# Attention of a two-layer backbone: a projection group moved to a scores bank, the context weights transposed ahead of the value products, all weight parts copied through SBUF in units with value products, and the head norms put off by a unit

## The chip, the cores and the metric

The kernel runs on one core of a Trainium2 chip. Its engines are TensorE (PE; its weight loads are listed as PEld), VectorE (DVE), ScalarE (ACT), GpSimd (POOL) and SyncE (SP), which issues the DMAs. Each has its own instruction stream and works it off in order; semaphores tie the streams together. The metric is the time of one execution on the device in microseconds (us), as the median of several runs.

## The reference

Two layers over 1024 latent tokens and 256 context tokens of width 1024. Layer 0 mixes tokens with differential attention, layer 1 with a state-space scan; each is followed by a dense MLP. The change touches layer 0's attention alone. For each of 8 heads there are two components c of width 64, and the two softmaxes are subtracted:

```python
s = einsum('bqhcd,bkhcd->bhcqk', q, k)
p = softmax(s, axis=-1)
w = p[:, :, 0] - lam * p[:, :, 1]
o = einsum('bhqk,bkhe->bqhe', w, v)
return rmsnorm(o, subln_g) * (1.0 - lambda_init)
```

q and k of the latent tokens are rotated (axial rotary) after their projections. Latent queries read all 1280 keys, context queries only the 256 context keys. All arithmetic is float32; the kernel multiplies in halves, hi and lo, with three products for one (`mm3`, L132 to L134).

## The kernel before, in words

**Tiling.** `phase_b` walks through 72 units (h, u): 8 heads of 9 units. In u=0 both 128-token tiles of context queries are done against 256 keys, in u=1 to 8 one latent tile each against 1280 keys. Around the units the order of TensorE, VectorE, ScalarE and GpSimd is the order in which the code is written (`manual_schedule`); the DMAs on SP are placed by a planner.

**One unit.** TensorE computes the scores of both components into PSUM banks 0 to 4 (`scores`, L510; L504 in u=0). VectorE copies each component to SBUF and takes its maximum on the way (`maxima`, L523; L519 in u=0; the instruction works with negated scores, so its accumulator is a minimum). ScalarE takes the exponentials with their sums (`exps`, L533; L530 in u=0), component 0 in a double buffer, component 1 in a single one. VectorE then forms w from both (`combine`, L541 to L544). One unit later TensorE transposes w in three parts, of 4, 2 and 4 key tiles (`w_part`, L556; for the context unit one part of 4 transposes, L551): part 0 into bank 5, part 1 into the upper half of bank 6, part 2 into bank 5 where the unit has a projection group and bank 7 where not. `w_evac` brings a part to SBUF as hi and lo: directly (ScalarE copies hi out of PSUM, L564; VectorE subtracts for lo out of PSUM, L565), or by one ScalarE copy to SBUF (L569, a ring of three buffers) from which GpSimd makes hi (L570) and lo (L571). Before, part 0 went the direct way, and parts 1 and 2 the other.

**Values.** Two units of latent tiles make a pair. Its value products (`values`, 30 matmuls of 256 columns; 6 for the context pair) into bank 6 stand right behind the scores of the unit two after the pair's last one: u=2 for the context pair and u=4, 6, 8 and the next head's u=1 for the four latent pairs. Those four are called late units here: the products read the weights that the unit's own parts are about to overwrite, so all three parts are evacuated only behind `combine`. `pair_out` (L652) copies the product out at the unit's end.

**Projections.** The next head's K and Q are projected in groups (`proj_group`) beside the units: two groups in u=0 (context keys, then the first latent keys), one each in u=2, 3, 5 and 7. All go to bank 7. Of u=0's two, the first is computed whole ahead of the scores and leaves bank 7 by ScalarE and VectorE (L451, L452); other groups' matmuls are spread between the transposes. A latent group has five further steps: `evac` (L456, L457, and four DMAs that swap rows), a step of nothing, `sine` (GpSimd, L462), `add` (VectorE, L465), `store` (ScalarE L137 and VectorE L138, both helpers that others use too, and two DMAs). Two steps are taken per unit, one in the middle (ahead of component 1's exponentials) and one at the end.

**Norms.** The rows of a finished head are normalised while the next one runs: `norm_load` fetches a pair's outputs and its broadcast row scales by two DMAs (tiles W, from od and rsd) at a unit's start, and `norm_pair` scales them at the unit's end (VectorE L684), splits them (ScalarE L137, GpSimd L138) and stores both halves. That is done in u=6, 7, 8 and the next head's u=0 and 1, from head 1's u=6 to head 7's u=1, with one set of buffers.

## Time and profile before

| | us |
|---|---|
| Median of three runs | 3051.51 (3049.69 to 3059.32) |
| The profiled execution's own time | 3048.01 |
| Its span on the core | 3046.2 |
| Heads and units of attention | from about 242 to 910 |

The mean granted TensorE clock is 0.978. The page's 40 slices are 76 us each; attention fills slices 4 to 12. The four heads between 425 and 760 us repeat each other closely, about 83 us per head, and head 4 (from its u=0 near 551 us) stands for them. In the tables of waits, a row reads: engine, tile and line that waited, the engine, tile and line whose end released it, total us, how many times, the longest. In a timeline, a row has its start, its length, engine, line, operation, output tile and input tile, shapes and count, and in square brackets the idle time of the engine before it with what ended that. A wait that depends on several things is put down to the one that came last.

### The profile page before, as it was taken

How to read it: one execution, taken by the hardware profiler on the slowest of the kernel's cores; microseconds unless marked ns; L12 is line 12 of the kernel's file. 1: busy time of each engine (PE TensorE's matmuls, PEld its weight loads, DVE VectorE, ACT ScalarE, POOL GpSimd, SP SyncE). 2: the span in 40 equal slices, each digit the busy share in tenths (PEclk: the TensorE clock that was granted, in tenths of full speed). 3: DMA queues.
4: the chain of work that ended last, by engine and by line, in shares of the span. 5: the costliest groups of instructions: out<-in, count | busy, mean ns of one | idle time of the engine just before them, and what ended most of it. 6: DMA issues, size and time to landing. Idle time of an engine off the chain costs nothing.

```text
span 3046.2 us, 42172 instructions
## 1 busy us (share of the span) xinstructions
PE 2855.1 (94%) x15376; PEld 2368.6 (78%) x15376; DVE 1909.6 (63%) x2766; ACT 1256.1 (41%) x2254; POOL 814.1 (27%) x794
## 2 busy tenths in 40 slices
PE   6998999999799999999999999688999899999998
PEld 4687888878687877788777778588787778888887
DVE  5357877777654654344677755899543666666555
ACT  3425555555544643333422222467344533222223
POOL 2314665666654400000100003566112200000003
PEclk9999999999899999999999999899999999999999
DMA  9955556556716455532666663577642221111113
GB/s 264 304 174 164 150 161 167 164 161 173 245 57 197 125 169 174 166 119 93 199 192 184 185 196 104 159 213 206 214 148 95 66 66 56 52 49 52 56 39 135
DMA packets 384235, 448.83 MB, mean 147 GB/s; under 512 B 54694, under 2 KB 299676, under 8 KB 382876
## 3 DMA queue, kind: packets, MB, share of 16 engines
q1 hardware_dynamic: 384028, 446.14, 49.1%
q8 instruction: 121, 1.98, 0.3%
q14 instruction: 86, 0.70, 0.1%
HBM read 320.88 MB, written 120.95 MB: 145 GB/s over the span
## 4 chain that ended last, share of the span: by engine, by line
PE 66%; DVE 10%; DMA 8%; issue 5%; ACT 4%; POOL 4%; SPq 3%; DVEq 0%; POOLq 0%; ACTq 0%
PE PS L132 19%; PE PS L134 19%; PE PS L133 19%; SPq L80 3%; PE PS L510 2%; ACT F L533 1%; PE PS L202 1%; DVE F L523 1%; DVE FD L1708 1%; PE PS L556 1%; PE PS L1690 1%; PE PS L1725 1%; DMA W<-rsd 1%; DVE FD L1699 1%; DVE R L138 1%
## 5 line engine op out<-in xcount | busy, mean ns | idle before, releaser
L132 PE MATMUL PS<-H,R 128*128 128x512 f32 (+1 forms) x960 | 361.3, 378 | 15.5 <-ACT F L569 13.8
L133 PE MATMUL PS<-H,R 128*128 128x512 f32 (+1 forms) x992 | 366.1, 369 | 2.9 <-POOL H L138 2.8
L134 PE MATMUL PS<-H,R 128*128 128x512 f32 (+1 forms) x960 | 348.9, 368 | 0.1
L133 PE MATMUL PS<-R,H 128*128 128x512 f32 x692 | 271.0, 392 | 0.0
L132 PE MATMUL PS<-R,H 128*128 128x512 f32 x676 | 268.2, 400 | 2.0 <-ACT R L137 1.6
L134 PE MATMUL PS<-R,H 128*128 128x512 f32 x676 | 260.1, 392 | 1.1 <-DVE H L138 1.1
L132 PE MATMUL PS<-R 128*128 128x256 f32 (+1 forms) x656 | 221.9, 339 | 7.0 <-ACT R L137 2.8
L132 PEld LDWEIGHTS PS<-H,R 128*128 128x128 f32 x960 | 184.3, 192 | 50.3 <-ACT F L569 15.2
L137 ACT ACTIVATE R<-W 128x512 fp32r<-128x512 f32 (+1 forms) x203 | 154.6, 766 | 161.1 <-PE PS L133 112.0
L1625 POOL TENSOR_SCALAR stat<-stat 128x1 f32<-128x1 f32 x24 | 14.9, 620 | 765.4 <-ACT PS L1623 765.1
L133 PE MATMUL PS<-R 128*128 128x256 f32 (+1 forms) x624 | 208.6, 334 | 9.1 <-DVE R L565 9.1
L1428 DVE TENSOR_TENSOR F<-PS,F 128x1024 f32<-128x1024 f32 (+1 forms) x113 | 136.4, 1212 | 128.3 <-PE PS L134 128.1
L133 PEld LDWEIGHTS PS<-H,R 128*128 128x128 f32 x992 | 191.4, 193 | 31.1 <-POOL H L138 3.6
L138 DVE TENSOR_TENSOR R<-W,R 128x512 fp32r<-128x512 f32 (+1 forms) x162 | 140.5, 872 | 114.5 <-ACT R L137 75.2
L134 PEld LDWEIGHTS PS<-H,R 128*128 128x128 f32 x960 | 184.3, 192 | 32.6 <-issue 2.1
L533 ACT ACTIVATE F<-F,stat 128x1280 f32<-128x1280 f32 x128 | 174.4, 1362 | 84.5 <-DVE F L523 84.2
L523 DVE TENSOR_SCALAR_CACHE_REDUCE F<-PS 128x1280 f32<-128x1280 f32 x128 | 185.1, 1483 | 8.6 <-PE PS L510 8.3
L570 POOL TENSOR_SCALAR R<-F 128x256 fp32r<-128x256 f32 (+1 forms) x128 | 124.2, 970 | 169.3 <-ACT F L569 147.5
L134 PE MATMUL PS<-R 128*128 128x512 f32 (+1 forms) x488 | 168.4, 354 | 0.0
L132 PE MATMUL PS<-H 128*128 128x512 f32 x408 | 161.0, 395 | 1.5 <-ACT H L137 1.5
L134 PE MATMUL PS<-H 128*128 128x512 f32 x408 | 159.4, 392 | 0.0
L510 PE MATMUL PS<-R,R 128*128 128x512 f32 x720 | 155.3, 364 | 0.4 <-DVE F L523 0.4
(426 smaller groups left out, 7037.8 us busy)
## 6 DMA issues: line engine op xcount, KB each, us to landing
W<-in_mlp_w SPq DMA_DIRECT2D x148, 256.0 KB
W<-in_mlp_w SPq DMA_DIRECT2D x68, 512.0 KB
FU<-in_ada_w SPq DMA_DIRECT2D x40, 512.0 KB
W<-in_ada_w SPq DMA_DIRECT2D x32, 512.0 KB
H<-hidd SPq DMA_DIRECT2D x64, 256.0 KB
W<-in_s_w_glu SPq DMA_DIRECT2D x64, 256.0 KB
hidd<-FU SPq DMA_DIRECT2D x52, 256.0 KB
recd<-FD SPq DMA_DIRECT2D x48, 256.0 KB
```

The source lines that it names most:

```text
L80: return self.nc.sync.dma_start(out=out, in_=in_)
L132: mm(out, ah, bh, start=first, stop=False, **kw)
L133: mm(out, ah, bl, start=False, stop=False, **kw)
L134: mm(out, al, bh, start=False, stop=last, **kw)
L137: self.nc.scalar.activation(hi, src, AF.Copy)
L138: (lo_eng or self.nc.vector).tensor_tensor(lo, src, hi.bitcast(F32), ALU.subtract)
L202: self.nc.tensor.matmul(acc[32 * j : 32 * j + 32, 0:256], self.scT[:, 2 * k : 2 * k + 32], w[:, 256 * j : 256 * j + 256], start=k == 0, st ...
L510: mm(self.PS[:, 1280 * c + k0 : 1280 * c + k1], Q[:, c, r, qs], K[c][:, k0:k1], start=r == 0, stop=r == 1)
L523: ts(p[c], self.PS[:, 1280 * c : 1280 * c + 1280], 1.0, None, ALU.mult, ALU.min, accum_out=sm[:, c : c + 1])
L533: nc.scalar.activation(p[c], p[c], AF.Exp, bias=sm[:, c : c + 1], scale=-1.0, accum_out=sn[:, 0:1] if c else s0[:, u + 1 : u + 2])
L570: nc.gpsimd.tensor_scalar(hi, t, 1.0, 0.0, ALU.mult, ALU.add)
L1428: nc.vector.tensor_tensor(acc[:, n : n + m], y[:, n : n + m], acc[:, n : n + m], ALU.add)
```

## The change

It has five parts.

1. In u=0 the first of the two projection groups is computed into bank 4, the last of the scores banks, in place of bank 7 (`proj_group` takes the bank as an argument).
2. In u=1, where w of the context unit is transposed (`first`), the transposes stand ahead of the 30 value products, the evacuation is direct, and it is placed right behind these products in the order, ahead of the exponentials.
3. In the other late units (u=4, 6, 8) part 0 also goes by one ScalarE copy and GpSimd (`part == 0 and (first or not late)`).
4. The empty step of a latent group is gone, and a step that was at a unit's end is put in `later` and taken in the next unit right behind the maxima. So `sine` comes at the next unit's middle, `add` behind the maxima of the unit after it, and `store` at that unit's middle. 
5. `norm_pair` also goes to `later`: behind the maxima of the next unit, behind a waiting `add`. `norm_load` moves from the unit's start to behind that.

TensorE, ScalarE and SP run the same number of instructions as before. On VectorE 24 subtractions (L565, 128x512) are gone; on GpSimd 24 pairs L570 and L571 of 128x512 are added. A few instructions of the output projection, behind attention, stand in another order, by the planner.

In the rows below, F_1811 is the buffer of w and its copies, R_98 and R_1810 hold rounded operands, FC the projection's and the norms' scratch, W the norms' and weights' staging, stat and lamc small columns, PS PSUM.

VectorE at u=2 of head 4, before, from the norm's scaling at the end of u=1 to the maxima of u=3:

```order
L684 SCALAR_TENSOR_TENSOR W<-W,lamc 128x256
L523 TENSOR_SCALAR F_1811,stat<-PS 128x1280 x2
L565 TENSOR_TENSOR R_98<-PS,R_98 128x4x128
L465 TENSOR_TENSOR FC<-FC 128x512
L541 RECIPROCAL stat<-stat 128x1
L542 SCALAR_TENSOR_TENSOR stat<-FC,stat,lamc 128x1
L544 SCALAR_TENSOR_TENSOR F_1811<-F_1811,stat 128x1280
L138 TENSOR_TENSOR R_98<-FC,R_98 128x512
L457 SCALAR_TENSOR_TENSOR FC<-PS,W 128x512
L523 TENSOR_SCALAR F_1811,stat<-PS 128x1280 x2
```

and now, from the maxima of u=2 to the end of that unit:

```order
L523 TENSOR_SCALAR F_1811,stat<-PS 128x1280 x2
L465 TENSOR_TENSOR FC<-FC 128x512
L684 SCALAR_TENSOR_TENSOR W<-W,lamc 128x256
L565 TENSOR_TENSOR R_98<-PS,R_98 128x4x128
L138 TENSOR_TENSOR R_98<-FC,R_98 128x512
L541 RECIPROCAL stat<-stat 128x1
L542 SCALAR_TENSOR_TENSOR stat<-FC,stat,lamc 128x1
L544 SCALAR_TENSOR_TENSOR F_1811<-F_1811,stat 128x1280
L457 SCALAR_TENSOR_TENSOR FC<-PS,W 128x512
```

The norm's L684 was ahead of the two maxima and is behind them, with the group's `add` (L465) ahead of it; the direct subtraction L565 comes behind both, and the store's L138 has moved from behind `combine` (L544) to ahead of it.

ScalarE from u=8 of head 3 to the exponentials of u=0 of head 4, before:

```order
L137 ACTIVATE W<-W 128x256
L533 ACTIVATE F_1811,FC<-F_1811,stat 128x1280
L533 ACTIVATE F_1811,stat<-F_1811,stat 128x1280
L564 ACTIVATE R_98<-PS 128x4x128
L569 ACTIVATE F_1811<-PS 128x256
L569 ACTIVATE F_1811<-PS 128x512
L652 ACTIVATE FC<-PS 128x256
L137 ACTIVATE W<-W 128x256
L451 ACTIVATE R_98<-PS 128x256
L564 ACTIVATE R_98<-PS 128x4x128
L530 ACTIVATE F_1811,FC<-F_1811,stat 128x256 x2
```

and now:

```order
L137 ACTIVATE W<-W 128x256
L533 ACTIVATE F_1811,FC<-F_1811,stat 128x1280
L533 ACTIVATE F_1811,stat<-F_1811,stat 128x1280
L569 ACTIVATE F_1811<-PS 128x512
L569 ACTIVATE F_1811<-PS 128x256
L569 ACTIVATE F_1811<-PS 128x512
L652 ACTIVATE FC<-PS 128x256
L451 ACTIVATE R_98<-PS 128x256
L137 ACTIVATE W<-W 128x256
L564 ACTIVATE R_98<-PS 128x4x128
L530 ACTIVATE F_1811,FC<-F_1811,stat 128x256 x2
```

Part 0 of u=8 is now an L569 like its neighbours, and the copy of the first group (L451) is ahead of the norm's L137 in place of behind it. The norm's L137 still stands ahead of the next exponentials, but it now reads what VectorE makes behind the maxima.

TensorE in u=1 of head 4, before, the last three value products, the context transposes and the next scores:

```order
L132 MATMUL PS<-R_98 128x256
L133 MATMUL PS<-R_98 128x256
L134 MATMUL PS<-R_98,R_1810 128x256
L551 MATMUL PS<-ident,F_1811 128x128 x4
L510 MATMUL PS<-R_1810,R_98 128x512 x4
L510 MATMUL PS<-R_1810,R_98 128x256 x4
L510 MATMUL PS<-R_1810,R_98 128x512 x4
L132 MATMUL PS<-R_98 128x256
```

and now, the end of u=0, the scores of u=1, the transposes and the first value products:

```order
L134 MATMUL PS<-H,R_98 128x512
L510 MATMUL PS<-R_1810,R_98 128x512 x4
L510 MATMUL PS<-R_1810,R_98 128x256 x4
L510 MATMUL PS<-R_1810,R_98 128x512 x4
L551 MATMUL PS<-ident,F_1811 128x128 x4
L132 MATMUL PS<-R_98 128x256
L133 MATMUL PS<-R_98 128x256
L134 MATMUL PS<-R_98,R_1810 128x256
```

The four transposes of the context weights (L551) have moved from behind the thirty value products to ahead of them.

The whole diff:

```diff
--- before.py
+++ after.py
@@ -428,11 +428,11 @@
 
         return split
 
-    def proj_group(self, h, T, g, wt):
+    def proj_group(self, h, T, g, wt, b=None):
 
         nc = self.nc
         n, c0 = self.G_TOK[g], (256, 768, 0)[g]
-        b = self.qb.next()[:, 0:n]
+        b = (self.qb.next() if b is None else b)[:, 0:n]
         scale = 1.0 if T else -0.125
         t = slice(c0 - 256, c0 + 256)
         hT = self.hT[g]
@@ -468,7 +468,7 @@
             self.split(s[:, 0], s[:, 1], qc)
             out()
 
-        return [product(k) for k in range(8)], [direct] if g == 2 else [evac, None, sine, add, store]
+        return [product(k) for k in range(8)], [direct] if g == 2 else [evac, sine, add, store]
 
 
     def lam_setup(self):
@@ -599,7 +599,7 @@
                 for f in post:
                     f()
                 rest[0]()
-                post = rest[2:]
+                post = rest[1:]
                 yield
         for f in post:
             f()
@@ -786,7 +786,7 @@
             if f:
                 f()
 
-        ready = []
+        ready, later = [], []
 
         def evac():
             while ready:
@@ -800,8 +800,6 @@
                 pv = todo.pop(0)[1:] if todo and todo[0][0] == n else None
                 late = pv and pv[1]
                 parts = 3 if prev and prev[1] else 1 if prev else 0
-                if front and n - 6 >= 9 and (n - 6) % 9 < 5 and (n - 6) // 9 < 7:
-                    norm_load((n - 6) // 9 - 1, (n - 6) % 9)
                 if h == 7 and u > 5:
                     load6(u)
                 if front:
@@ -816,7 +814,8 @@
                     if u % 2 == 0 and u < 8 and (h, pair + 1) not in loaded:
                         load_q(h, pair + 1)
                     if h < 7:
-                        groups = [self.proj_group(h + 1, *a, wts[a[0]]) for a in self.AHEAD.get(u, ())]
+                        ahead = self.AHEAD.get(u, ())
+                        groups = [self.proj_group(h + 1, *a, wts[a[0]], self.bank(4) if a != ahead[-1] else None) for a in ahead]
                     if len(groups) == 2:
                         for f in groups[0][0] + groups[0][1]:
                             f()
@@ -826,6 +825,10 @@
                         load_q(h + 1, 0)
                         load_q(h + 1, 1)
                     self.maxima(u, p, sm)
+                while later:
+                    later.pop(0)()
+                if front and n - 6 >= 9 and (n - 6) % 9 < 5 and (n - 6) // 9 < 7:
+                    norm_load((n - 6) // 9 - 1, (n - 6) % 9)
                 if front:
                     if h < 7:
                         if u == 0:
@@ -839,14 +842,17 @@
                     fills = [groups[0][0][i : i + 2] for i in (0, 2, 4)]
                 elif groups:
                     fills = [groups[-1][0][i:j] for i, j in (((0, 4), (4, 8), (8, 8)) if u == 3 else ((0, 3), (3, 6), (6, 8)))]
-                if pv:
+                first = parts == 1
+                if pv and not first:
                     values(*pv)
                 for part in range(3):
                     if part < parts:
                         tb = pb[:, 256:512] if part == 1 else self.bank(7 if part == 2 and not groups else 5)
                         t = self.w_part(prev[1], prev[2], part, tb)
-                        ready.append((*t, part == 0))
-                    if not late or part == 2:
+                        ready.append((*t, part == 0 and (first or not late)))
+                    if pv and first and part == 0:
+                        values(*pv)
+                    if not late or first or part == 2:
                         evac()
                     if part == 1:
                         next_post()
@@ -872,7 +878,8 @@
                     sums.append((n + 1, lambda a=pv: pair_sums(*a)))
                     if pv[0] == 7:
                         tail.append((n + 1, pv[1]))
-                next_post()
+                if post:
+                    later.append(post.pop(0))
                 if groups:
                     rest = groups[-1][1]
                     rest[0]()
@@ -894,7 +901,7 @@
                     elif u == 5:
                         norm_rows(h - 1)
                 if h < 8 and n - 6 >= 9 and (n - 6) % 9 < 5 and (n - 6) // 9 < 7:
-                    norm_pair((n - 6) // 9 - 1, (n - 6) % 9)
+                    later.append(lambda a=((n - 6) // 9 - 1, (n - 6) % 9): norm_pair(*a))
                 if n == 72:
                     self.raw = Ring([self.wv(8, 1024), self.wv(12, 1024)])
                     self.wo_raws = [self.wo_load(3, 0), self.wo_load(0, 1)]
```

## The prediction

> **What bounds the kernel now.** I read the table of TensorE's waits, that of 425 to 760 us (four heads), then the timelines of head 4. TensorE's waits that the change aims at, over the whole execution:
>
> ```profile
> PE PS L556 <- DVE R L565: 20.3, 14, 2.9
> PE PS L132 <- ACT F L569: 13.8, 6, 2.6
> ...
> PE PS L133 <- DVE R L565: 9.1, 6, 2.4
> ...
> PE PS L659 <- ACT F L569: 6.4, 1, 6.4
> ```
>
> Together 49.6 us: no removal of these waits is worth more. In head 4 they are found at u=0's first group, the context pair's values in u=2, and part 0 in u=5:
>
> ```profile
> 551.25 0.39 PE L132 MATMUL PS<-H,R 128*128 128x256 f32 x1 [2.54 <-ACT F L569]
> ...
> 573.93 0.39 PE L133 MATMUL PS<-R 128*128 128x256 f32 x1 [1.21 <-DVE R L565]
> ...
> 601.21 0.66 PE L556 MATMUL PS<-ident,F 128*128 128x128 f32 x4 [1.54 <-DVE R L565]
> ```
>
> The second thing to see is how little room the softmax leaves. In four heads VectorE waited 20.8 us for the norm's row scales, and its maxima 0.7 for scores:
>
> ```profile
> DVE W L684 <- DMA W<-rsd: 20.8, 11, 3.2
> ...
> DVE F L523 <- PE PS L510: 0.7, 4, 0.2
> ```
>
> So maxima, exponentials, `combine` and the next maxima form a chain as long as TensorE's work. The starts of the first maximum in u=8 of head 3, and in u=0, 1, 2, 3, 7 and 8 of head 4:
>
> ```profile
> 545.57 1.48 DVE L523 TENSOR_SCALAR_CACHE_REDUCE F<-PS 128x1280 f32<-128x1280 f32 x1
> ...
> 556.68 0.41 DVE L519 TENSOR_SCALAR_CACHE_REDUCE F<-PS 128x256 f32<-128x256 f32 x1
> ...
> 566.78 1.48 DVE L523 TENSOR_SCALAR_CACHE_REDUCE F<-PS 128x1280 f32<-128x1280 f32 x1
> ...
> 577.33 1.49 DVE L523 TENSOR_SCALAR_CACHE_REDUCE F<-PS 128x1280 f32<-128x1280 f32 x1
> ...
> 585.69 1.48 DVE L523 TENSOR_SCALAR_CACHE_REDUCE F<-PS 128x1280 f32<-128x1280 f32 x1
> ...
> 617.79 1.48 DVE L523 TENSOR_SCALAR_CACHE_REDUCE F<-PS 128x1280 f32<-128x1280 f32 x1
> ...
> 628.86 1.48 DVE L523 TENSOR_SCALAR_CACHE_REDUCE F<-PS 128x1280 f32<-128x1280 f32 x1
> ```
>
> The steps are 11.11, 10.10, 10.55, 8.36, 32.10 (four units) and 11.07 us, 83.3 together. I work the change out as new lengths of these steps.
>
> **The change part by part.** The pieces of a plain step, from u=4, and one L465 of each length, the long one with the GpSimd row beside it:
>
> ```profile
> 594.13 1.48 DVE L523 TENSOR_SCALAR_CACHE_REDUCE F<-PS 128x1280 f32<-128x1280 f32 x1
> 597.06 1.37 ACT L533 ACTIVATE F<-F,stat 128x1280 f32<-128x1280 f32 x1
> 600.47 0.68 DVE L565 TENSOR_TENSOR R<-PS,R 128x512 fp32r<-128x512 f32 x1
> 596.95 0.68 DVE L465 TENSOR_TENSOR FC<-FC 128x512 f32<-128x512 f32 x1
> 621.58 1.77 DVE L465 TENSOR_TENSOR FC<-FC 128x512 f32<-128x512 f32 x1 [0.29 <-POOL FC L462]
> 621.50 1.30 POOL L138 TENSOR_TENSOR R<-W,R 128x512 fp32r<-128x512 f32 x1
> ```
>
> The first exponential starts about 1.52 behind the first maximum's start, the second 1.41 later (597.06), and w is done 3.41 after that, as L565 follows it: 6.34. Both maxima take 2.82 (594.13 to 596.95). Now the norm around u=2:
>
> ```profile
> 576.92 0.49 DVE L684 SCALAR_TENSOR_TENSOR W<-W,lamc 128x256 f32<-128x256 f32 x1 [3.05 <-DMA W<-rsd]
> 577.49 0.42 ACT L137 ACTIVATE W<-W 128x256 fp32r<-128x256 f32 x1 [5.51 <-DVE W L684]
> 577.82 0.58 ACT L564 ACTIVATE R<-PS 128x512 fp32r<-128x512 f32 x1
> 582.62 0.64 ACT L137 ACTIVATE R<-FC 128x512 fp32r<-128x512 f32 x1
> 583.87 1.10 DVE L138 TENSOR_TENSOR R<-FC,R 128x512 fp32r<-128x512 f32 x1
> 544.23 1.42 DVE L684 SCALAR_TENSOR_TENSOR W<-W,lamc 128x256 f32<-128x256 f32 x1
> ```
>
> From L684's start to the end of ScalarE's copy: 0.90. Before, this ran ahead of the maxima, and the first exponential lay beside the second maximum. Now ScalarE, in order, holds the norm's copy ahead of the exponentials, and that copy needs L684 behind both maxima. The first exponential starts 2.82 + 0.90 = 3.72 behind the first maximum, 2.20 later than in a plain step; an `add` ahead of L684 costs 0.68 more, a direct copy (L564) behind it 0.58. This is the price of part 5; its return is that the norm and its wait for row scales leave the stretch ahead of the maxima. Step by step, in us:
>
> - u=8 to u=0, 11.11. 3.72 + 1.41 + 3.41, and 0.4 for the direct group's subtraction: 8.9, **−2.2**. Bank 4 pays here: the 2.54 for bank 7 go, since u=8's maxima are over at 548.4 (545.57 + 2.82) and TensorE could start at 548.7 (551.25 − 2.54).
> - u=0 to u=1, 10.10. L684 and the store's L138 (0.5 and 1.1) leave its end; `add`, L684, L137 and L564 delay its exponentials. 8.7 with short lengths, 10.7 where L465 and L684 take 1.77 and 1.42: **−0.4**, between.
> - u=1 to u=2, 10.55. 3.72 + 0.58 + 1.41 + 3.41 = 9.1: **−1.4**; the 3.05 for row scales go. Part 2 takes the 1.21 off TensorE here, but it then stands at u=2's part 0 until u=1's w is done, so it counts nothing by itself.
> - u=2 to u=3, 8.36. 3.72 + 0.68 + 0.58 + 1.41 + 3.41, between the exponentials 0.64 for the store's copy and 0.3 for a part's, and 0.6 for the cosine product: 11.3, **+3.0**.
> - u=3 to u=7, 32.10. No norm. In u=4 the store's copy now waits for `add`: 2.82 + 0.68 + 0.64 + 3.41 = 7.55, 0.4 less than now, as part 3 takes a 0.68 subtraction away from behind w; u=6's end loses such a subtraction and L684 (0.68 + 0.4). TensorE's work takes part of it: **−1.5**. The 1.54 at u=5 shrinks by those 0.68, no further, as w is late.
> - u=7 to u=8, 11.07. As u=2: 11.3; with GpSimd busy under L465 and L684 2.0 more: **+1.0**, half of it.
>
> Sum −1.5 per head. Bounds: all short −3.9 (−2.2, −1.35, −1.4, +3.0, −2.1, +0.2), all long +2.4 (−1.7, +0.6, −0.9, +3.0, −0.8, +2.2). I take the middle, as L465 shows both lengths.
>
> Part 3's GpSimd work is, in each of 24 units, one more pair like
>
> ```profile
> 784.06 0.62 POOL L570 TENSOR_SCALAR R<-F 128x512 fp32r<-128x512 f32 x1
> 784.77 1.29 POOL L571 TENSOR_TENSOR R<-F,R 128x512 fp32r<-128x512 f32 x1
> ```
>
> 1.9 us, about 46 in all. I cost it at nothing beyond the lengths above: its weights are read two units later, and `sine` moves ahead of it out of the same queue. If that cover fails, u=6's and u=8's values wait about 1 us each, which the upper bound holds.
>
> The moved steps pass other queues. `sine` now stands on GpSimd ahead of its unit's part copies and waits there for four row swaps; L570 and L571 queue behind it, for weights that are read a unit or more later, and I cost it at nothing for the same reason. On ScalarE everything of the unit queues behind the norm's copy: direct copy, exponentials, L569, `pair_out`; on VectorE, behind L684, the direct subtraction that frees bank 5 for part 2, and `combine`. On SP a norm is two stores and two loads:
>
> ```profile
> SPq L80 <- POOL W L138: 22.7, 8, 5.3
> ```
>
> SP stood 22.7 us before the lo stores, with swaps and query loads behind them, as GpSimd's L138 came last in its unit. Now L138 stands ahead of the unit's parts, and the row scales' load, which needs only L684, ahead of both stores. So I price SP at nothing, and expect the wait for row scales to shrink; if a store still blocks the output load, L684 waits for W<-od instead, by at most what it waited for row scales, 20.8 in 20 norms, 1 us each.
>
> Five rounds from head 1 to head 6 give 5 × −1.5 = −7.5. Head 0 to 1 has no norms: bank 4 saves about 1.0. Head 6 to 7 had the longest waits for row scales and, behind them, TensorE's 6.43:
>
> ```profile
> 788.21 0.48 DVE L684 SCALAR_TENSOR_TENSOR W<-W,lamc 128x256 f32<-128x256 f32 x1 [4.60 <-DMA W<-rsd]
> 809.75 0.71 DVE L684 SCALAR_TENSOR_TENSOR W<-W,lamc 128x256 f32<-128x256 f32 x1 [3.76 <-DMA W<-rsd]
> 813.78 0.98 PE L659 MATMUL PS<-lamc,adat 128*128 128x1 f32 x4 [6.43 <-ACT F L569]
> ```
>
> Row scales have a unit and its maxima to arrive now, but exponentials still queue behind them: I take 3 of the 6.4, bounds 0 and 6. Sum −7.5 − 1.0 − 3.0 = −11.5: 3048.0 − 11.5 = 3036.5 for an execution like the profiled one, which lies 3.5 below the median; so 3051.5 − 11.5 = **3040** as a median. Own range −26 (3025) to +11 (3062).
>
> **The rivals.**
>
> - *TensorE alone is the bound*, and the softmax has room. Then the 13.8, 9.1 and 6.4 go, and half of the 20.3: −39, 3012. For it: TensorE's share here. Against: the 0.7 us above. Chance 0.12.
>
> ```profile
> PE 2855.1 (94%) x15376; PEld 2368.6 (78%) x15376; DVE 1909.6 (63%) x2766; ACT 1256.1 (41%) x2254; POOL 814.1 (27%) x794
> ```
>
> - *Slower: the exponentials pay.* Norm and `add` stand between maxima and exponentials in five of nine units. If L465 and L684 mostly meet a running GpSimd instruction, a round costs +2.4: six rounds +14, 3066. It decides from the point where they lose 1.5 us per round more than I took. For it: the L465 at 621.58 ended 0.6 behind the GpSimd row that began just before it, and part 3 gives GpSimd more to do in u=6. Against: both lengths are there already. Chance 0.17.
> - *Nothing gained:* what bank 4 saves in u=0 is given back in u=2 and u=7. For it: the sum ends at 2% of its round. 3051, chance 0.28.
>
> [...]
>
> **How the numbers follow.** Chances: forecast 0.43, the others 0.12, 0.17, 0.28. A measurement can tell about 0.3%, 9 us, from no change: faster is below 3042.4, slower above 3060.7. The forecast's case ends below 3042.4 five times in six: faster 0.36 + 0.12 = 0.48, same 0.07 + 0.27 = 0.34, slower 0.18. The range, 3018 to 3062, leaves out most of the first rival and the far end of the second, about 0.2.
>
> **What would show it.** Right: TensorE's wait at u=0's first group under 1 us; `L133 <- L565` gone; VectorE's wait for row scales well under 20 us; steps u=2 to u=3 and u=7 to u=8 above 11, u=8 to u=0 near 9. Wrong: rounds of 83 us or more with values that wait for L570 and L571, or rounds near 77 us, if TensorE was the bound.

## The result, and the profile after

The changed kernel takes 3066.18 us as the median of six runs (3065.38 to 3068.03), beside 3050.60 (3042.13 to 3059.42) for the kernel before in the same session: ratio 1.0053, interval 1.0036 to 1.0069. It is slower, by about 16 us, where 11.5 us less had been predicted. Its profiled execution took 3065.38 us with a span of 3063.4, 17.2 more than the 3046.2 of before. The page's line of busy times:

```profile
PE 2867.3 (94%) x15376; PEld 2368.0 (77%) x15376; DVE 1895.7 (62%) x2742; ACT 1249.1 (41%) x2254; POOL 857.2 (28%) x842
```

VectorE has its 24 instructions less and 14 us of work less, GpSimd 48 more and 43 us of work more, as the change says. TensorE's waits over the whole execution, the rows that answer to those of before:

```profile
PE PS L556 <- DVE F L544: 27.0, 15, 4.3
...
PE PS L556 <- DVE R L565: 13.9, 15, 2.4
...
PE PS L132 <- ACT FC L652: 9.9, 5, 4.7
```

The waits that parts 1 and 2 aim at are gone: `L132 <- L569` (13.8 before) and `L133 <- L565` (9.1). In their place stands a row that came to 1.4 us before: the transposes now wait 27.0 us for w itself (L544). What TensorE no longer waits for banks and weights, it waits for the softmax. The first maxima from u=8 of head 3 to u=8 of head 4 (u=8, 0, 1, 2, 3, 7, 8), VectorE's timeline:

```profile
555.13 1.48 DVE L523 TENSOR_SCALAR_CACHE_REDUCE F<-PS 128x1280 f32<-128x1280 f32 x1
...
563.90 0.41 DVE L519 TENSOR_SCALAR_CACHE_REDUCE F<-PS 128x256 f32<-128x256 f32 x1
...
575.29 1.48 DVE L523 TENSOR_SCALAR_CACHE_REDUCE F<-PS 128x1280 f32<-128x1280 f32 x1
...
584.49 1.48 DVE L523 TENSOR_SCALAR_CACHE_REDUCE F<-PS 128x1280 f32<-128x1280 f32 x1
...
595.40 1.48 DVE L523 TENSOR_SCALAR_CACHE_REDUCE F<-PS 128x1280 f32<-128x1280 f32 x1
...
628.68 1.49 DVE L523 TENSOR_SCALAR_CACHE_REDUCE F<-PS 128x1280 f32<-128x1280 f32 x1 [0.57 <-PE PS L510]
...
640.71 1.48 DVE L523 TENSOR_SCALAR_CACHE_REDUCE F<-PS 128x1280 f32<-128x1280 f32 x1
```

| step, head 4 (us) | before | predicted | after |
|---|---|---|---|
| u=8 to u=0 | 11.11 | 8.9 | 8.77 |
| u=0 to u=1 | 10.10 | 9.7 | 11.39 |
| u=1 to u=2 | 10.55 | 9.1 | 9.20 |
| u=2 to u=3 | 8.36 | 11.3 | 10.91 |
| u=3 to u=7 | 32.10 | 30.6 | 33.28 |
| u=7 to u=8 | 11.07 | 12.1 | 12.03 |
| sum | 83.3 | 81.8 | 85.6 |

Four of the six steps came out within 0.4 of the forecast. The other two went the wrong way, by 1.7 and 2.7. By the first maxima of the heads (before: 235.98 for head 0, 309.06 for head 1, 722.83 for head 6, 810.39 for head 7; after: 236.32, 310.10, 737.52, 823.83), head 0 got 0.7 longer, heads 1 to 5 13.65 (2.7 each), head 6 1.25 shorter, and 3.8 came behind the start of head 7: its units up to u=8 got 6.9 longer, and what follows them 3.2 shorter.

**The two steps that failed.** In u=0 (ScalarE's and VectorE's timelines of head 4):

```profile
565.28 0.79 DVE L465 TENSOR_TENSOR FC<-FC 128x512 f32<-128x512 f32 x1
567.11 0.90 DVE L684 SCALAR_TENSOR_TENSOR W<-W,lamc 128x256 f32<-128x256 f32 x1 [1.05 <-DMA W<-od]
...
568.09 0.42 ACT L137 ACTIVATE W<-W 128x256 fp32r<-128x256 f32 x1 [4.69 <-DVE W L684]
568.41 0.58 ACT L564 ACTIVATE R<-PS 128x512 fp32r<-128x512 f32 x1
568.89 0.50 ACT L530 ACTIVATE F<-F,stat 128x256 f32<-128x256 f32 x1
...
573.14 1.62 DVE L544 SCALAR_TENSOR_TENSOR F<-F,stat 128x256 f32<-128x256 f32 x1
```

The first exponential starts at 568.89, 4.99 behind the first maximum. Between them stand `add`, a wait of 1.05 for the outputs' load, the scaling, ScalarE's copy for it, and the direct copy. At the unit's end the second L544 takes 1.62 in place of the 0.48 that it took before; it runs beside an L571 of GpSimd (573.19 to 574.49). From u=3 to u=6 two other things are at work. In u=3, VectorE beside GpSimd:

```profile
600.23 1.00 DVE L542 SCALAR_TENSOR_TENSOR stat<-FC,stat,lamc 128x1 f32<-128x1 f32 x1
601.26 1.97 DVE L544 SCALAR_TENSOR_TENSOR F<-F,stat 128x1280 f32<-128x1280 f32 x1
...
603.49 0.93 DVE L665 TENSOR_TENSOR FC<-FC 128x10 f32<-128x10 f32 x1
...
599.93 1.27 POOL L462 TENSOR_TENSOR FC<-FC,W 128x512 f32<-128x512 f32 x1
601.27 0.62 POOL L570 TENSOR_SCALAR R<-F 128x512 fp32r<-128x512 f32 x1
601.98 2.41 POOL L571 TENSOR_TENSOR R<-F,R 128x512 fp32r<-128x512 f32 x1
```

The sine product (L462), which the change moved here, ends at 601.20; L542, an instruction on one column, ends at 601.23 and took 1.00 us, before 0.22. L544 and L665 took 1.97 and 0.93, before 1.55 and 0.24. L667 behind them fell from 1.15 to 0.17, so the step as a whole grew by 0.9. In u=4 the store's copy waits for `add`, ahead of the second exponential, and TensorE stands for w at u=5's part 0:

```profile
608.33 0.63 ACT L137 ACTIVATE R<-FC 128x512 fp32r<-128x512 f32 x1 [0.61 <-DVE FC L465]
608.87 1.35 ACT L533 ACTIVATE F<-F,stat 128x1280 f32<-128x1280 f32 x1
...
610.80 1.55 DVE L544 SCALAR_TENSOR_TENSOR F<-F,stat 128x1280 f32<-128x1280 f32 x1
...
612.50 0.63 PE L556 MATMUL PS<-ident,F 128*128 128x128 f32 x4 [2.21 <-DVE F L544]
```

### The profile page after: what moved, and what is told of

Read it like the earlier page. It is cut to its first block, busy times and chain, and to the rows that moved or that the text cites. A ratio compares the mean times of both kernels' runs of the same rounds, so it can differ in the third digit from the quotient of the medians.

```text
span 3063.4 us, 42271 instructions
## 1 busy us (share of the span) xinstructions
PE 2867.3 (94%) x15376; PEld 2368.0 (77%) x15376; DVE 1895.7 (62%) x2742; ACT 1249.1 (41%) x2254; POOL 857.2 (28%) x842
## 4 chain that ended last, share of the span: by engine, by line
PE 71%; DVE 7%; DMA 6%; POOL 5%; ACT 4%; issue 3%; SPq 2%; DVEq 0%; ACTq 0%; POOLq 0%
PE PS L132 21%; PE PS L134 21%; PE PS L133 21%; PE PS L510 2%; SPq L80 2%; PE PS L202 2%; POOL R L570 1%; PE PS L556 1%; POOL R L571 1%; PE PS L1732 1%; PE PS L1697 1%; DVE FD L1715 1%; DMA W<-od 1%; ACT F L533 1%; DVE F L523 1%
## 5 line engine op out<-in xcount | busy, mean ns | idle before, releaser
L133 PE MATMUL PS<-H,R 128*128 128x512 f32 (+1 forms) x992 | 364.4, 367 | 2.9 <-POOL H L138 2.8
L132 PE MATMUL PS<-H,R 128*128 128x512 f32 (+1 forms) x960 | 360.6, 377 | 1.7 <-ACT R L137 1.1
L133 PE MATMUL PS<-R,H 128*128 128x512 f32 x692 | 272.5, 394 | 0.0
L132 PE MATMUL PS<-R,H 128*128 128x512 f32 x676 | 268.6, 400 | 1.9 <-ACT R L137 1.6
L132 PE MATMUL PS<-R 128*128 128x256 f32 (+1 forms) x656 | 222.8, 340 | 15.3 <-ACT FC L652 9.9
L137 ACT ACTIVATE R<-W 128x512 fp32r<-128x512 f32 (+1 forms) x203 | 154.8, 768 | 161.2 <-PE PS L133 111.9
L133 PEld LDWEIGHTS PS<-H,R 128*128 128x128 f32 x992 | 189.7, 191 | 31.4 <-POOL H L138 3.6
L138 DVE TENSOR_TENSOR R<-W,R 128x512 fp32r<-128x512 f32 (+1 forms) x162 | 140.5, 872 | 117.8 <-ACT R L137 76.9
L132 PEld LDWEIGHTS PS<-H,R 128*128 128x128 f32 x960 | 182.8, 191 | 35.2 <-issue 5.4
L133 PE MATMUL PS<-R 128*128 128x256 f32 (+1 forms) x624 | 208.0, 333 | 0.2 <-POOL R L571 0.2
L523 DVE TENSOR_SCALAR_CACHE_REDUCE F<-PS 128x1280 f32<-128x1280 f32 x128 | 185.3, 1484 | 10.7 <-PE PS L510 10.3
L571 POOL TENSOR_TENSOR R<-F,R 128x512 fp32r<-128x512 f32 (+1 forms) x152 | 182.5, 1200 | 12.7
L132 PE MATMUL PS<-H 128*128 128x512 f32 x408 | 161.2, 395 | 2.3 <-ACT H L137 1.8
L570 POOL TENSOR_SCALAR R<-F 128x512 fp32r<-128x512 f32 (+1 forms) x152 | 132.5, 871 | 108.3 <-ACT F L569 94.5
```

The costliest lines, as they stand in the source:

```text
L132: mm(out, ah, bh, start=first, stop=False, **kw)
L133: mm(out, ah, bl, start=False, stop=False, **kw)
L137: self.nc.scalar.activation(hi, src, AF.Copy)
L138: (lo_eng or self.nc.vector).tensor_tensor(lo, src, hi.bitcast(F32), ALU.subtract)
L523: ts(p[c], self.PS[:, 1280 * c : 1280 * c + 1280], 1.0, None, ALU.mult, ALU.min, accum_out=sm[:, c : c + 1])
L570: nc.gpsimd.tensor_scalar(hi, t, 1.0, 0.0, ALU.mult, ALU.add)
```

## The experiments

Two theories came out of this. **A:** part 5 costs, as ScalarE holds the norm's copy ahead of the exponentials. **B:** part 4 costs, by the two things just shown. All kernels compute the whole reference. The time is the median, and the ratio is to the kernel before in the same session (3050.6 us for the change, then 3050.9, 3049.2 and 3049.6 in three sessions of experiments). SP's DMAs are placed by the planner anew for each kernel, so kernels that differ in one part can differ in that order as well.

| parts | us | ratio (interval) |
|---|---|---|
| 1 to 5 (the change) | 3066.2 | 1.0053 (1.0036, 1.0069) |
| 1 to 4 | 3054.9 | 1.0015 (1.0006, 1.0025) |
| 5 alone | 3065.3 | 1.0052 (1.0035, 1.0068) |
| 1 alone | 3039.3 | 0.9973 (0.9956, 0.9990) |
| 1, 2, 3, 5 | 3061.5 | 1.0039 (1.0025, 1.0054) |
| 1, 2 | 3032.6 | 0.9957 (0.9940, 0.9974) |
| 1, 2, 3 | 3053.4 | 1.0013 (1.0003, 1.0024) |
| 1, 4 | 3063.3 | 1.0052 (1.0037, 1.0067) |
| 1, 2, 4 | 3053.4 | 1.0016 (1.0004, 1.0028) |
| 1, and the sine products early | 3055.7 | 1.0024 (1.0015, 1.0034) |
| 1, 2, 5 | 3057.9 | 1.0030 (1.0021, 1.0040) |
| 1, 2, norm beside the exponentials | 3021.9 | 0.9917 (0.9901, 0.9933) |
| 1 to 4, norm beside the exponentials | 3047.8 | 0.9994 (0.9985, 1.0003) |

### The norm taken back, and the norm alone

Against the changed kernel:

```diff
+                if front and n - 6 >= 9 and (n - 6) % 9 < 5 and (n - 6) // 9 < 7:
+                    norm_load((n - 6) // 9 - 1, (n - 6) % 9)
                 if h == 7 and u > 5:
                     load6(u)
...
-                if front and n - 6 >= 9 and (n - 6) % 9 < 5 and (n - 6) // 9 < 7:
-                    norm_load((n - 6) // 9 - 1, (n - 6) % 9)
...
-                    later.append(lambda a=((n - 6) // 9 - 1, (n - 6) % 9): norm_pair(*a))
+                    norm_pair((n - 6) // 9 - 1, (n - 6) % 9)
```

> The changed kernel with part 5 undone: norm_load again at the unit's start, norm_pair at its end; parts 1 to 4 stay. Theory A (the norm between maxima and exponentials is what costs): the step from u=2 to u=3 falls from 10.9 to about 8.5 us, u=7 to u=8 from 12.0 to about 9.5, a round from 85.6-88.5 to 80-82, and the time to about 3035, faster than the kernel before. Theory B (the moved steps of part 4 and GpSimd's extra parts cost): the steps from u=3 to u=6 keep their 26.3 (24.4 before), a round stays at 83 us or more, the time at 3050 or above.

Measured: 3054.9. And part 5 on the kernel before, the same lines with signs turned round:

> The kernel before with part 5 alone: the norm behind the next unit's maxima. Theory A: u=2 to u=3 grows from 8.4 to 10.5-11, u=7 to u=8 from 11.1 to 12.5 or more, while u=1 to u=2 falls to about 9.2; round 85-88, time 3062-3072. Theory B: the round stays within 1 us of 83, time 3045-3055.

Measured: 3065.3. So part 5 costs about 12 us as the last part and 14 as the only one. Alone, it makes longer the very wait that bank 4 removes (TensorE's waits from 230 to 900 us, part 5 alone):

```profile
PE PS L132 <- ACT F L569: 26.7, 6, 5.1
```

ScalarE's copy that frees bank 7 queues behind the put-off norm and the exponentials of u=8: 26.7 us in place of 13.8. But the kernel without part 5 is no faster than the kernel before (1.0015), where A alone had said 3035. In head 4 of it u=2 to u=3 falls to 8.1, as A said (8.5), while u=3 to u=6 stays at 26.5 as B said, and u=7 to u=8 at 12.25, where A had said 9.5. So A is not the whole.

### The bank, and the context weights

Part 1 on the kernel before, then part 2 on top:

```diff
-    def proj_group(self, h, T, g, wt):
+    def proj_group(self, h, T, g, wt, b=None):
...
-        b = self.qb.next()[:, 0:n]
+        b = (self.qb.next() if b is None else b)[:, 0:n]
...
-                        groups = [self.proj_group(h + 1, *a, wts[a[0]]) for a in self.AHEAD.get(u, ())]
+                        groups = [self.proj_group(h + 1, *a, wts[a[0]], self.bank(4) if a != self.AHEAD[u][-1] else None) for a in self.AHEAD.get(u, ())]
```

> The kernel before with part 1 alone: the first group of u=0 in bank 4. By the prediction's own term, TensorE's 2.5 us at u=0 go in each head and, with them, up to 1.5 us at half clock behind that wait in some heads: round about 81, time about 3037. The rival (given back later in the round): the wait moves to u=2's part 0 or u=5's part 0, round 83, time 3050.

```diff
-                if pv:
+                first = parts == 1
+                if pv and not first:
                     values(*pv)
...
+                    if pv and first and part == 0:
+                        values(*pv)
-                    if not late or part == 2:
+                    if not late or first or part == 2:
                         evac()
```

> The kernel before with parts 1 and 2 alone (first group in bank 4, context transposes ahead of the values with a direct evacuation); copies in units with values, steps and norms as before. Bank 4 alone measured 3039.3. Theory 'part 2 counts nothing by itself': the 1.2 us that TensorE stood in u=2 for the context weights' lo goes, but u=2's part 0 then waits for u=1's w; step u=1 to u=2 stays near 9.9 and the time is 3036 to 3042. Rival 'part 2 is worth its whole wait': step u=1 to u=2 falls to about 8.7, 7 x 1.2 = 8 us less, 3031.

Measured: 3039.3 and 3032.6. Part 1 gains about 11 us. The half clock named in its expectation is seen in head 4 of the kernel before: behind the wait of 2.54, by 1 us from 551 to 556, the granted clock was 0.81, 0.50, 0.50, 0.50 and 0.98. Part 2 gains some 5 more by the medians (the intervals overlap in part). The context weights' wait (L133 for L565, 9.5 us from 230 to 900 us) goes, but TensorE's wait for w (L556 for L544) grows from 1.4 to 8.2, as the prediction had said. The step from u=0 to u=1 in heads 2 to 6 ends at 8.7 to 9.4 us, from 9.1 to 10.0 with part 1 alone, while u=1 to u=2, the step that had been named, stays near 9.8. The time lies between the two expectations, and where the gain arises is not shown: of the 5.9 us between the two profiled spans, heads 0 to 6 hold only 2.5.

### The copies

Part 3 on parts 1 and 2, one line:

```diff
-                        ready.append((*t, part == 0))
+                        ready.append((*t, part == 0 and (first or not late)))
```

> Parts 1, 2 and 3 (part 3: part 0 also by one ScalarE copy and GpSimd in units with values), steps and norms as before. Theory of the prediction: 24 subtractions of 0.68 us leave VectorE behind combine, and in u=5 part 0 can start that much earlier, about 0.7 us per head: 4 to 5 us less than with parts 1 and 2 alone. Rival 'GpSimd's backlog': with L570 and L571 of 1.9 us more in a unit, values and store wait for GpSimd: as slow as or slower than parts 1 and 2 alone, by up to 1 us per unit with values, +10 us.

Measured: 3053.4, 21 us more. The step from u=4 to u=5 does shrink, from 7.97 to 7.36, by the subtraction taken away. But the two steps behind it grow by 0.7 and 0.8, u=0 to u=1 grows to 11.0 to 12.0, and u=7 to u=8 from 11.08 to 12.25 in most heads. VectorE's `add` in u=7 and in u=0 of this kernel, and waits of TensorE from 230 to 900 us:

```profile
625.36 1.76 DVE L465 TENSOR_TENSOR FC<-FC 128x512 f32<-128x512 f32 x1 [1.01 <-POOL FC L462]
...
563.59 1.22 DVE L465 TENSOR_TENSOR FC<-FC 128x512 f32<-128x512 f32 x1 [1.61 <-POOL FC L462]
```

```profile
PE PS L504 <- DMA R<-Kd: 10.3, 5, 2.9
...
PE PS L133 <- POOL R L571: 4.9, 6, 1.0
```

In u=7 GpSimd's 1.9 us more put the sine product off, behind it `add` waits 1.0 us and then runs beside GpSimd (1.76 in place of 0.68). The step follows that wait: 11.75 here, and 12.25 in heads 3 and 5, where `add` waits 1.5. In u=0 `add` waits too (1.61, then 1.22), but something else lies beside it: TensorE's scores now wait for the key load, 10.3 us in all, and the step from u=0 to u=1 grew by 11.0 over heads 2 to 6. SP's rows show why, first with parts 1 and 2, then with part 3:

```profile
535.50 0.32 SPq L80 DMA_DIRECT2D R<-Kd  x1
```

```profile
554.71 0.86 SPq L80 DMA_DIRECT2D R<-Kd  x2
```

The first maximum of u=8 is at 538.85 and 550.17. So one of two key loads, which SP had issued 3.4 us ahead of u=8's maxima, now stands 4.5 behind them, together with the other and behind the norm's stores; in heads 2 to 6 it is alike. This order is the planner's. No run keeps the order and adds the copies, so how much of the 21 us belongs to the copies themselves is not shown. The value products' own wait for L571 is a small part, 4.9.

### The steps

Part 4 taken out of the change:

```diff
-        return [product(k) for k in range(8)], [direct] if g == 2 else [evac, sine, add, store]
+        return [product(k) for k in range(8)], [direct] if g == 2 else [evac, None, sine, add, store]
...
-                if post:
-                    later.append(post.pop(0))
+                next_post()
```

> The changed kernel with part 4 undone: the empty step is back, sine and add at their old places; parts 1, 2, 3 and 5 stay. Theory A: no sum ahead of the norm any more, so u=2 to u=3 and u=7 to u=8 lose about 0.7 each, but 10 and 11 us remain; time 3058-3066. Theory B: u=3 to u=4 back at 8.4 (from 9.3), u=4 to u=6 at 16.0 or less (from 16.9), round 83 or less, time 3050 or less.

Measured: 3061.5, so part 4 costs some 5 us as the last part (the intervals overlap). u=3 to u=4 falls back to 8.44 and u=3 to u=7 of head 4 to 31.5, but u=0 to u=1 grows to 12.8 to 13.9 in heads 2 to 6, and u=2 to u=3 and u=7 to u=8 keep their 11.0 and 12.3. Those are thus not made by `add` ahead of the norm. Then part 4 on part 1 (the signs turned round), and on parts 1 and 2:

> Parts 1 and 4 (a latent group's steps with the empty one gone and the end step taken behind the next unit's maxima), without parts 2, 3 and 5. Theory B (the projections' steps in their new places cost, by the store's ScalarE copy that waits for the add ahead of the second exponential, and by the sine products beside combine): steps u=3 to u=4 near 9.4 in place of 8.44 and u=5 to u=6 near 9.4 in place of 7.96, +2 us per head, 3039 + 13 = 3052. Rival (they cost only together with the delayed norm, as the changed kernel without part 4 was but 4.7 us faster): 3039 to 3042.

> Parts 1, 2 and 4. Part 4 cost 24 us on part 1 alone, but 1.5 us on parts 1, 2 and 3. This tells which of parts 2 and 3 takes its cost away. Theory 'part 3' (part 3's GpSimd backlog already holds the steps u=5 to u=8 and u=0 long, and part 4, whose sine stands earlier on GpSimd, relieves it): part 4 still costs its steps u=3 to u=4 and u=5 to u=6 here, 3032.6 + 20 = 3052. Rival 'part 2' (it was the context weights' late evacuation together with the store's copy ahead of the second exponential in u=2 that cost): 3034 to 3042.

Measured: 3063.3 and 3053.4, 26 and 20 us more than without part 4, each taken against its own session's kernel before. u=3 to u=4 is 9.57 in every one of heads 1 to 6, u=5 to u=6 9.0 to 11.7: theory B, and larger than it said. The longest single wait lies in u=0, where ScalarE of the second kernel shows

```profile
562.83 0.63 ACT L137 ACTIVATE R<-FC 128x512 fp32r<-128x512 f32 x1 [4.87 <-DMA Kd<-R]
563.37 0.49 ACT L530 ACTIVATE F<-F,stat 128x256 f32<-128x256 f32 x1
```

The store, moved to the unit's middle, writes the tile that the context keys' store is still reading, and component 1's exponentials wait behind it: 4.87 us, and a step of 13.1. But most of that comes back in the next step, which falls to 7.1 from 9.9: over heads 2 to 6 u=0 costs 13.1 us more than with parts 1 and 2, and u=1 gives 11.7 back. What lasts is u=3 and u=5 (5.6 and 10.9), less 4.3 and 7.6 in u=6 and u=7. Last, the sine products alone in their earlier place, on part 1:

```diff
-        return [product(k) for k in range(8)], [direct] if g == 2 else [evac, None, sine, add, store]
+        return [product(k) for k in range(8)], [direct] if g == 2 else [evac, sine, None, add, store]
...
-                post = rest[2:]
+                post = rest[1:2] + rest[3:]
```

> Part 1 with one piece of part 4: the sine products in the place of the empty step, at the next unit's middle, an empty step where they were; add and store as before. Theory B1 (of part 4, the sine products beside combine cost: the step u=3 to u=4 grows from 8.4 to about 9.5 as VectorE's small operation and combine wait beside GpSimd): +1.1 us per head, 3039.3 + 7 = 3046, and bank_steps' other 17 us belong to the store's copy ahead of the second exponential. Rival: the sine products early save add its wait and gain, 3030 to 3038, and the store carries all of part 4's cost.

Measured: 3055.7, 18 us more than part 1 alone where 7 were expected. The mechanism is as told: u=3 to u=4 is 9.7 to 9.8 in four of six heads, 8.5 in the other two. In head 4, L542 beside the sine product, and with it in its old place:

```profile
592.65 1.18 DVE L542 SCALAR_TENSOR_TENSOR stat<-FC,stat,lamc 128x1 f32<-128x1 f32 x1
...
592.52 1.29 POOL L462 TENSOR_TENSOR FC<-FC,W 128x512 f32<-128x512 f32 x1
```

```profile
593.73 0.22 DVE L542 SCALAR_TENSOR_TENSOR stat<-FC,stat,lamc 128x1 f32<-128x1 f32 x1
...
589.12 1.29 POOL L462 TENSOR_TENSOR FC<-FC,W 128x512 f32<-128x512 f32 x1
```

Both of the first pair end at 593.8. But 1.2 us in four heads is not 18. Over heads 2 to 6, u=0 to u=1 and u=2 to u=3 are longer too (3.7 and 2.3 us), while u=7 to u=8 is 4.3 shorter; what makes them so was not followed further.

### The place of the norm

Part 5 on parts 1 and 2; then, on the same kernel, the norm put off just as far but to the middle of the next unit:

```diff
-                if front and n - 6 >= 9 and (n - 6) % 9 < 5 and (n - 6) // 9 < 7:
-                    norm_load((n - 6) // 9 - 1, (n - 6) % 9)
...
                         self.exps(u, part, p, sm, s0, sn)
                     if front and part == 1:
+                        if norms:
+                            norm_pair(*norms.pop())
+                        if n - 6 >= 9 and (n - 6) % 9 < 5 and (n - 6) // 9 < 7:
+                            norms.append(((n - 6) // 9 - 1, (n - 6) % 9))
+                            norm_load(*norms[0])
                         self.combine(u, p, s0, sn)
...
-                if h < 8 and n - 6 >= 9 and (n - 6) % 9 < 5 and (n - 6) // 9 < 7:
-                    norm_pair((n - 6) // 9 - 1, (n - 6) % 9)
```

> Parts 1, 2 and 5: the bank and the context weights as changed, and the norm put off to right behind the next unit's maxima as in the change; copies and steps as before. It differs from the norm beside the exponentials (3021.9) only in where the put-off norm stands, and from parts 1 and 2 alone (3032.6) only in part 5. Theory A (the place costs, not the delay: ScalarE's copy for the norm ahead of both exponentials): as part 5 alone cost 15 us on the kernel before, 3032.6 + 15 = 3048. Rival (with the bank and the context weights in place the put-off norm gains, and its place matters little): 3022 to 3033.

> Parts 1 and 2, and the norm put off too, but to the middle of the next unit: behind component 1's maxima and the first exponential, ahead of combine, so that ScalarE's copy for the norm stands behind component 0's exponential and not ahead of it; norm_load right behind. Theory A (part 5 costs because ScalarE, in order, holds the norm's copy ahead of both exponentials, not because the norm is late): the wait for row scales leaves the stretch ahead of the maxima and the first exponential stays 1.5 us behind the first maximum; steps u=1 to u=2 near 8.5, u=7 to u=8 near 10, 3015 to 3032. Rival (any put-off of the norm costs, as its copy still stands ahead of the second exponential or its row scales come no earlier): 3037 to 3055.

Measured: 3057.9 and 3021.9. The two kernels issue the same work and put the norm off by the same unit; 36 us lie in its place, and the second is the fastest of all, 27 us below the kernel before. In u=1 of head 4, VectorE and ScalarE with part 5:

```profile
570.24 1.48 DVE L523 TENSOR_SCALAR_CACHE_REDUCE F<-PS 128x1280 f32<-128x1280 f32 x1
...
573.62 0.42 ACT L137 ACTIVATE W<-W 128x256 fp32r<-128x256 f32 x1 [6.44 <-issue]
...
574.42 1.35 ACT L533 ACTIVATE F<-F,stat 128x1280 f32<-128x1280 f32 x1
```

and with the norm in the middle of the unit:

```profile
556.42 1.48 DVE L523 TENSOR_SCALAR_CACHE_REDUCE F<-PS 128x1280 f32<-128x1280 f32 x1
...
559.84 0.48 DVE L684 SCALAR_TENSOR_TENSOR W<-W,lamc 128x256 f32<-128x256 f32 x1
...
563.26 1.48 DVE L523 TENSOR_SCALAR_CACHE_REDUCE F<-PS 128x1280 f32<-128x1280 f32 x1
```

```profile
557.95 1.36 ACT L533 ACTIVATE F<-F,stat 128x1280 f32<-128x1280 f32 x1 [1.47 <-DVE F L523]
...
559.42 1.37 ACT L533 ACTIVATE F<-F,stat 128x1280 f32<-128x1280 f32 x1
...
560.78 0.40 ACT L137 ACTIVATE W<-W 128x256 fp32r<-128x256 f32 x1
```

With part 5 the first exponential starts 4.18 behind the first maximum, here 1.53. The scaling runs while VectorE has nothing to do but wait for exponentials, ScalarE's copy comes behind both of them, and the step is 6.84 us, from 9.92 with the norm in its old place and 9.20 with part 5. u=8 to u=0 is 7.72 (10.9 and 9.4). Over heads 2 to 6 the two kernels differ by 30.0 us, of which the steps of u=7, u=8 and u=1 hold 28.1. VectorE's scaling, GpSimd's part and SP's loads moved along with ScalarE's copy, and no run moves the copy alone. It is not all gain: u=0 to u=1 and u=2 to u=3 are 12.5 and 10.8, from 9.2 and 8.4. In u=2 the scaling, which now stands ahead of `combine`, waits for the outputs, and in u=0 of head 5 the group's store again waits for the key store:

```profile
569.75 0.48 DVE L684 SCALAR_TENSOR_TENSOR W<-W,lamc 128x256 f32<-128x256 f32 x1 [2.39 <-DMA W<-od]
```

```profile
634.63 0.63 ACT L137 ACTIVATE R<-FC 128x512 fp32r<-128x512 f32 x1 [3.51 <-DMA Kd<-R]
```

So a put-off norm has a price of its own, in the DMAs. Last, the norm in the same place in the changed kernel, with all its other parts:

> The changed kernel with the put-off norm beside the exponentials: the norm stands at the middle of the next unit, behind the first exponential, not right behind the maxima; parts 1 to 4 as changed. Theory A (part 5 costs by its place ahead of the exponentials): at or below the changed kernel with its norm in place (3054.9), by as much as the same move gained on parts 1 and 2 (11 us): 3044. Rival (with GpSimd's and ScalarE's queues as full as in the change, a put-off norm cannot gain wherever it stands): 3055 to 3066.

Measured: 3047.8, 17 us below the change and 6 below its parts 1 to 4, where 11 were expected. Theory A holds there too, with a smaller gain than on parts 1 and 2.

### Why the parts do not add up

By the medians, each against its own session's kernel before, parts 3, 4 and 5 cost 21, 20 and 25 us each on parts 1 and 2. Together they cost 32, and as the last to be added 5 (part 4) and 12 (part 5). The step from u=0 to u=1 shows a good part of it. In heads 2 to 6 it is 8.7 to 9.4 us with parts 1 and 2, 11.0 to 12.0 with part 3, 10.9 to 13.1 with part 4, 12.9 with part 5, and 11.4 to 12.9 with all of them. The step behind it gives some of that back, so both are summed here, over heads 2 to 6 of the profiled executions:

| on parts 1 and 2 (us) | part 3 | part 4 | part 5 | all three |
|---|---|---|---|---|
| u=0 to u=2 | 5.2 | 1.4 | 16.2 | 11.2 |
| all steps | 8.4 | 7.6 | 20.9 | 21.4 |

In all steps the three come to 36.9 one by one and 21.4 together, and 11.6 of these 15.5 lie in u=0 to u=2. Each part brings a wait of its own in u=0 (TensorE for the key load, ScalarE for the key store, ScalarE for the scaling), but the rows show them beside one another in time: whichever ends last sets the step. In the change, ScalarE is held until 568.09 for the norm; of waits like that of 4.87 us, the table of the four heads has one of 0.5 left for the store's copy, and TensorE's wait for the key load is gone. u=7 to u=8 is alike: 11.1 with parts 1 and 2, 12.25 with part 3, 12.4 with part 5, 12.0 with all. Which part would have to go first cannot be read from the change alone.

## Why the prediction was wrong, step by step

**Wrong: u=3 to u=7, −1.5 forecast, +1.2 measured.** Two sentences of it failed. The sine products' move was priced at nothing, since they wait only for swaps and what queues behind them is wanted later. What was left out is that VectorE runs beside them: L542, L544 and L665 of u=3 lengthen by 1.9 together (L667 shortens by 1.0), and u=3 to u=4 went from 8.44 to 9.34. With part 4 taken out it is 8.44 again. And "the 1.54 at u=5 shrinks by those 0.68, no further" had the wrong sign. The step of u=4 came out as worked out (7.53, forecast 7.55), but it is measured from maximum to maximum. TensorE waits for w, and w came 7.53 us behind the first maximum (what follows it on VectorE starts at 612.27, the maximum at 604.74) in place of 6.34, since the second exponential stood behind `add` and the store's copy. The wait at u=5 grew from 1.54 to 2.21 and the step of u=5 from 7.96 to 9.41: what the chain's own step saved, the engine that follows it lost a unit later.

**Wrong: u=0 to u=1, −0.4 forecast, +1.3 measured (1.1 to 2.1 in heads 2 to 6).** Of the pieces, the direct copy and the norm's copy are as priced. Two terms were missing. One is the 1.14 by which the second L544 lengthens beside GpSimd's L571; `combine` had no long length in the sum. The other is the wait of 1.05 for the outputs' load; it had been named under the DMAs, with 1 us as its bound, but as a bound and not in this step, and in heads 2 to 6 it occurs in this step alone:

```profile
DVE W L684 <- DMA W<-od: 5.5, 4, 2.5
```

Four times in four heads (425 to 760 us), 1.4 each. The forecast's 8.7 with short lengths, these two, and the 0.53 that L465 and L684 took beyond their short lengths come to 11.42, and 11.39 was measured. The wait for row scales, 20.8 before, has no row left in that table, as forecast.

**Right in size: the other four steps.** u=8 to u=0 (8.77 for 8.9), u=1 to u=2 (9.20 for 9.1), u=2 to u=3 (10.91 for 11.3) and u=7 to u=8 (12.03 for 12.1). The working of u=2, the first exponential at 3.72 + 0.68 + 0.58 = 4.98 behind the first maximum at 584.49, is seen in ScalarE's rows, 4.78 behind:

```profile
588.47 0.42 ACT L137 ACTIVATE W<-W 128x256 fp32r<-128x256 f32 x1 [5.94 <-issue]
588.79 0.58 ACT L564 ACTIVATE R<-PS 128x512 fp32r<-128x512 f32 x1
589.27 1.35 ACT L533 ACTIVATE F<-F,stat 128x1280 f32<-128x1280 f32 x1
```

For u=2 the cause is shown too: without part 5 its step is 8.1. For u=7 it is not: that step is 12.25 without part 5 as well, so the right number there is partly luck. Bank 4's gain stands in size, as part 1 alone is faster by 11 us, but alone it lies in u=0 to u=1 and u=1 to u=2 (5.0 and 3.4 over heads 2 to 6), and u=8 to u=0, where the forecast had put it, keeps its length.

**Wrong in size: the ends.** Head 0 was to save 1.0 and lost 0.7: part 1 alone saves 0.9 there, and part 4 on parts 1 and 2 takes 3.4. Head 6 to 7 was to save 3; head 6 saved 1.25, and from head 7 on 3.8 were lost, with TensorE's waits of 4.33, 4.70 and 4.72 us in its first units (824 to 847 us). The forecast looked at one wait of 6.43 there and not at what would follow it.

**Part 3's "nothing" is not borne out**, and only the experiments show it: 21 us on parts 1 and 2. The bound given, 1 us at the values of u=6 and u=8, looked at the consumer of the copies. In u=7 the cost fell on `add`, which waits for the sine product that GpSimd does behind them. In u=0 it fell on the key load, which the planner issued later; the forecast had priced SP at nothing. In the change itself TensorE has no wait for that load.

**The sum.** The forecast says that it takes the middle of its bounds, but the middle of −3.9 and +2.4 is −0.75, and it took −1.5, the sum of its steps. With the middle the five rounds would have given −3.8 in place of −7.5.

**The rivals.** "The exponentials pay" gave 3066, and its place is right: part 5's cost is its place ahead of the exponentials, as 3057.9 against 3021.9 shows. Its mechanism was L465 and L684 beside GpSimd. In u=7 and u=0 of head 4 they took 0.79, 1.51, 0.79 and 0.90, or 1.7 us more than their short lengths (0.68 and 0.48), out of 6.3 between the forecast's bounds of −3.9 and +2.4, and less than the 2.4 that its −1.5 held for it. So the 2.7 per round came from the terms above, and the agreement of the sum is partly chance. The forecast had not looked at u=3, where L542, L544 and L665 of head 4 took 1.00, 1.97 and 0.93 beside GpSimd, before 0.22, 1.55 and 0.24. "TensorE alone is the bound" fell. "Nothing gained" (3051) was right that u=2 and u=7 lengthen, by 2.6 and 1.0 in head 4, but u=0 and u=3 to u=7 came on top. The sign of being wrong that the forecast had named came by half: the rounds are over 83 us, but the values wait for L571 only once, 0.2 us.

## What to carry to other kernels

When work is put behind the maxima of a softmax, look at what every engine has queued between maxima and exponentials: 36 us lay between two places of the same put-off norm, one with ScalarE's copy ahead of the exponentials and one with it behind them. A step measured from one engine's instruction to its next can shrink while its product comes later, so follow the product (here w) to the engine that waits for it. And time the parts of a change apart: of five, two gained 17 us together and the other three each cost 20 or more on top of them, yet the whole was only 16 us slower, in good part since their waits lie beside one another. When a part's time surprises, compare the order of the DMAs too: with part 3 one key load had moved by 8 us.

## What the runs showed of the hardware

**Instructions on one column and on ten were longer beside GpSimd too.** In u=3 of head 4, L542, 128x1, took 0.22 us in its usual place, and beside GpSimd's L462 1.00 in the changed kernel and 1.18 with part 1 and the sine products early, ending within 0.03 us of it; L665, 128x10, took 0.93 in place of 0.24 and ended with an L571, which in its turn had taken 2.41 in place of 1.29 beside L544. The prediction had looked only at wide instructions.

**The clock was halved after a wait of 2.2 us in heads 3 and 5, and not in head 4.** TensorE's wait at u=5 was alike in head 3 and head 4 of the changed kernel (2.22 and 2.21). TensorE's windows in and after it (start and end, length, busy time and instructions, granted clock, DMA share, GB/s), two of head 3 and two of head 4:

```profile
524.00:527.00 3.00, 1.47 (x6) 0.73 0.74 184
527.00:530.00 3.00, 3.00 (x12) 0.70 0.67 208
...
611.00:614.00 3.00, 1.50 (x9) 1.00 0.91 188
614.00:617.00 3.00, 3.00 (x16) 1.00 0.58 201
```

In head 3 the granted clock has a mean of 0.73 and 0.70 in these windows, and 3 us held 12 instructions in place of 16; in head 4 it stayed at 1.00. Taken by 1 us from 525 to 530, it was 0.69, 0.50, 0.50, 0.60 and 1.00; what these lack of 1.00 adds up to 1.71 us, as at half clock for 3.4 us. That step took 10.55 us in head 3 and 9.41 in head 4. Head 5, with a wait of 2.21 and windows of 0.74 and 0.69, took 10.65. That is 1.1 and 1.2 us more than in head 4, about half the wait's own length again. Why the same wait was followed by half the clock in two heads and not in the third is not shown.
